# A four-layer streaming trunk on one core: where the first layer's norm comes from, where the convolution's sums lie, and a new table for the planned order

## Chip, core and metric

The kernel runs on one core of a Trainium2 chip. The metric is the device time of one execution in microseconds; lower is better. Shown are the median of three runs and one execution taken apart by the hardware profiler. The engines are TensorE (PE; weight loads are shown apart as PEld), VectorE (DVE), ScalarE (ACT), GpSimd (POOL) and SyncE (SP), which issues the DMAs.

## What is computed

x is 512 frames by 1024 channels in float32. Four layers each add a mixer's output to x: differential attention, a Conformer convolution module, latent attention, and differential attention again. Cut to what the change touches:

```python
def _rms_norm(x, g):
    y = x * lax.rsqrt(jnp.mean(x * x, axis=-1, keepdims=True) + NORM_EPS)
    return y * g

def _conformer_conv(h, w_in, b_in, conv_w, conv_b, ln_g, ln_b, w_out):   # h = _rms_norm(x, g)
    a, b, gate = jnp.split(h @ w_in + b_in, 3, axis=-1)
    u = a * jax.nn.sigmoid(b)
    u = depthwise_causal_conv(u, conv_w) + conv_b        # 31 taps, per channel
    u = jax.nn.silu(_layer_norm(u, ln_g, ln_b))
    return (u * jax.nn.silu(gate)) @ w_out
```

Products of the large matrices are computed in three matmuls with each operand split into a high and a low part (Hh and Hl for x times the norm's gain).

## The kernel before

**Layout.** X holds x with channels on partitions, as 8 blocks of 128 channels by 512 frames. The norm's factor per frame, rs, is not multiplied into Hh and Hl: projections are made of x times the gain, and rs (and its square rs2) is applied to the results, where they leave PSUM or in the sums of squares of q and k.

**The order of the work.** The program is written as nodes (Plan, L363). Each node names its engine, an estimated cost and the buffers that it reads and writes. `Plan.order` (L576) then runs through a model of the engines: at each step, of the nodes that are ready it takes the one that can start first, and among equals the one with the lowest priority number. That number is the place in the program plus a shift, and the table SHIFT (L210 to L353) gives a further shift for each kind of node ("L1_c5.pe=-1835" moves the matmuls of block 5's convolution in layer 1 ahead by 1835 places). What comes out is one fixed sequence of instructions for each engine; on the chip each engine runs its sequence in order and waits on semaphores.

**Buffers.** SLOTS (L53) lists kinds of buffers with their number. A kind marked True is handed out in the order in which the program names them, whoever is ready. For PSUM there are four banks "pp" (True), three banks "x" (False, free for all) and one "o". For SBUF, "mid" has four, "wt" two, "p" two and "big" two.

**Layer 0, `start` (L834).** The four tiles of 128 frames of x are loaded into two "big" buffers, transposed by PE into "x" banks, scaled by the gain into Hh (ACT), copied to X (ACT) and the low part made in Hl (DVE). Then `norm_block` (L881) squares each of the eight blocks of X on ACT (L_sq) and adds them up on POOL (L_sqs); `norm_end` (L895) sums over partitions with matmuls by ones into a bank "o" (L_ss), and a reciprocal square root on POOL gives rs. The rope tables' setup is the next user of the "big" buffers.

**Layer 1, `layer_b` (L1158).** `glu_chunk` (L1204) makes a and b of one or two channel blocks in the four pp banks. The b half is multiplied by R (rs spread over partitions) into SBUF and put through the sigmoid. The a half is multiplied by R out of PSUM into SBUF (into L_ab_v for blocks of kind Y, into u itself otherwise); a second operation adds the bias and multiplies by the sigmoid (L1219, L1223).

KINDS (L30) 'DPDPDYYY' says who sums the 31 taps of each of the eight blocks. D: DVE, 30 operations on a bank "x" (L1236). P: ACT multiplies and POOL adds (L1253). Y: `conv_phase` (L1289) on PE: u is moved by 16 DMAs within SBUF into another layout (L_u4, L1297), DVE builds four weight tiles (L_wa, two buffers "p"), and PE sums into an accumulator of the kind "pp" (L_c). The memset of L_u4 takes the accumulator's bank, and the first matmul comes after the moves.

The gate's channels follow in two chunks of four blocks in the pp banks (L1312), and the program names the three convolution accumulators between them (L1343 to L1347). Behind all stands the LayerNorm over the eight blocks (L_stat, L_mv, L_lnr_y), the transposes back (L_ytr, L1366) and the output projection.

Of the kernel before, what the change touches and what calls it, by code (L numbers as in the profile page):

```python
# [1635 lines left out]
```

## Time and profile before

| | us |
|---|---|
| median of three runs | 1061.58 |
| lowest and highest | 1061.21, 1062.21 |
| the profiled execution | 1064.24 |
| its span, first to last instruction | 1062.4 |
| POOL busy | 216.0 |
| ACT busy | 586.1 |

Lines of the profile read: start, duration, engine, line of the kernel, operation, written tile <- read tiles, shapes and count; in square brackets how long the engine stood idle before, and what ended it. A helper's line stands for all that call it (L465 is every matmul, L519 every DVE operation of two tensors, L531 every operation of a tensor, a scalar and a tensor), so tiles tell more than lines. Layer and buffer numbers are left out of the names: L_c is any layer's c tiles. A row of a group reads: line, engine, operation, tiles, shape and count | busy us in all, mean ns of one | idle us before them and what ended it.

### The profile page before, as it was taken

Reading aid. Unit: us, or ns where it says so; the run is one execution under the profiler, and the core shown is the slowest. Engines: PE = TensorE matmul, PEld = TensorE weight load, DVE = VectorE, ACT = ScalarE, POOL = GpSimd, SP = SyncE. Lnnn points to the kernel's source line nnn. Section 1 sums busy time; section 2 is a strip of 40 time slices with the busy share of each in tenths; the row PEclk is TensorE's granted clock in tenths of the full one; section 3 lists DMA queues with packets and bytes.
Section 4 is the critical chain, followed back from the end, with each engine's and each line's share of the span. In section 5 each row is a group of like instructions: output and inputs, shape, how many; then the busy total and the mean of one; then the engine's idle time right before and its main releaser. Section 6 shows DMA issues by size and latency. Waiting matters only on the chain.

```text
span 1062.4 us, 15183 instructions
## 1 busy us (share of the span) xinstructions
PE 1010.8 (95%) x5212; PEld 847.7 (80%) x5212; DVE 764.4 (72%) x1966; ACT 586.1 (55%) x1226; POOL 216.0 (20%) x142
## 2 busy tenths in 40 slices
PE   8899999998999999798999999999999999999798
PEld 6688788887887887687887778788878888887687
DVE  4767689795669998768344769964683699989651
ACT  6557266657644556653343667753443746666642
POOL 3500000000012899960530001000210000000000
PEclk9999999998999999999999999999999999999899
DMA  7252241314014332220222211112232514423102
GB/s 240 83 138 61 80 119 60 100 48 117 31 51 128 110 104 87 79 91 1 58 91 65 85 50 60 41 38 80 80 100 85 153 41 119 112 68 101 39 20 80
DMA packets 74309, 87.53 MB, mean 82 GB/s; under 512 B 17110, under 2 KB 47702, under 8 KB 74233
## 3 DMA queue, kind: packets, MB, share of 16 engines
q1 hardware_dynamic: 74232, 86.57, 27.5%
q8 instruction: 41, 0.67, 0.3%
q14 instruction: 36, 0.29, 0.1%
HBM read 75.28 MB, written 2.10 MB: 73 GB/s over the span
## 4 chain that ended last, share of the span: by engine, by line
PE 70%; POOL 8%; ACT 8%; DVE 5%; issue 4%; DMA 2%; SPq 2%; DVEq 0%; ACTq 0%; POOLq 0%
PE L_o L465 21%; PE L_qk_a L465 15%; PE L_g_a L465 10%; PE L_v_a L465 7%; PE L_ab_a L465 5%; POOL L_cq L522 4%; POOL L_sqs L522 2%; ACT G L495 1%; SPq L569 1%; PE L_c_a L465 1%; PE L_qk_tr L471 1%; PE L_h7j_sc L465 1%; PE L_h2j_sc L465 1%; PE L_h6j_sc L465 1%; DMA L_setup<-a_lam_k 1%
## 5 line engine op out<-in xcount | busy, mean ns | idle before, releaser
L465 PE MATMUL L_qk_a<-L_qk_w,Hh 128*128 128x512 f32 x512 | 163.1, 400 | 2.6 <-DVE L_qk_T L519 1.3
L465 PE MATMUL L_o<-L_y,L_o_w 128*128 128x512 f32 x576 | 143.3, 398 | 0.3 <-DVE L_y L531 0.2
L465 PEld LDWEIGHTS L_o<-L_y,L_o_w 128*128 128x128 f32 x576 | 105.7, 189 | 21.9 <-DVE L_y L519 0.9
L465 PE MATMUL L_g_a<-L_g_w,Hh 128*128 128x512 f32 x384 | 120.8, 396 | 1.2 <-DVE L_g_w L519 0.5
L745 POOL TENSOR_TENSOR L_h_or_y<-L_h_ov,minus_half 128x4 f32<-128x4 f32 x16 | 17.5, 1093 | 465.9 <-DVE L_h_ov L540 302.3
L465 PEld LDWEIGHTS L_qk_a<-L_qk_w,Hh 128*128 128x128 f32 x512 | 91.9, 189 | 19.6 <-DVE L_qk_T L519 1.5
L465 PE MATMUL L_qk_a<-L_qk_w,Hl 128*128 128x512 f32 x256 | 100.6, 393 | 2.0 <-DVE Hl L531 2.0
L522 POOL TENSOR_TENSOR L_cq<-L_cq,L_ct 128x512 f32<-128x512 f32 x58 | 84.9, 1463 | 24.7 <-ACT L_ct L495 20.7
L465 PE MATMUL L_v_a<-L_v_w,Hh 128*128 128x512 f32 x256 | 82.5, 404 | 2.1 <-DVE L_qk_T L519 2.1
L465 PEld LDWEIGHTS L_g_a<-L_g_w,Hh 128*128 128x128 f32 x384 | 70.2, 188 | 15.9 <-DVE L_g_w L519 0.9
L465 PE MATMUL L_ab_a<-Hh,L_ab_w 128*128 128x512 f32 x256 | 80.1, 391 | 0.0
L465 PE MATMUL L_g_a<-L_g_w,Hl 128*128 128x512 f32 x192 | 75.2, 391 | 0.0
L522 POOL TENSOR_TENSOR L_sqs<-L_sqs,L_sq 128x512 f32<-128x512 f32 x28 | 45.4, 1620 | 130.5 <-ACT L_sq L495 129.1
L531 DVE SCALAR_TENSOR_TENSOR L_c<-L_u,L_tab,L_c 128x512 f32<-128x512 f32 x90 | 65.6, 749 | 1.5
L519 DVE TENSOR_TENSOR L_g_w<-L_g_w_r,L_g_w 128x1024 fp32r<-128x1024 f32 x32 | 43.5, 1360 | 28.9 <-ACT L_g_w L502 28.8
L495 ACT ACTIVATE L_ct<-L_u,L_tab 128x512 f32<-128x512 f32 x60 | 43.0, 722 | 35.1 <-POOL L_cq L522 35.0
L465 PEld LDWEIGHTS L_qk_a<-L_qk_w,Hl 128*128 128x128 f32 x256 | 48.1, 188 | 13.6 <-DVE Hl L531 3.3
L502 ACT CAST L_g_w<-L_g_w_r 128x1024 fp32r<-128x1024 f32 x32 | 33.6, 1050 | 41.7 <-PE L_v_a L465 22.0
L465 PEld LDWEIGHTS L_ab_a<-Hh,L_ab_w 128*128 128x128 f32 x256 | 48.1, 188 | 10.1
L465 PEld LDWEIGHTS L_v_a<-L_v_w,Hh 128*128 128x128 f32 x256 | 46.8, 192 | 11.6 <-DVE L_qk_T L519 2.6
L502 ACT CAST L_qk_w<-L_qk_w_r 128x1024 fp32r<-128x1024 f32 (+1 forms) x33 | 33.7, 1037 | 36.3 <-PE L_o L465 14.6
L465 PE MATMUL L_v_a<-L_v_w,Hl 128*128 128x512 f32 x128 | 50.9, 398 | 0.0
(366 smaller groups left out, 2335.6 us busy)
## 6 DMA issues: line engine op xcount, KB each, us to landing
L_qk_w_r<-a_w_in SPq DMA_DIRECT2D x62, 256.0 KB, 3.0
L_v_w_r<-a_w_in SPq DMA_DIRECT2D x16, 512.0 KB, 3.8
L_g_w_r<-a_w_in SPq DMA_DIRECT2D x16, 512.0 KB, 3.7
L_qk_st<-L_qk_st SPq DMA_DIRECT2D x32, 256.0 KB, 4.3
L_o_w_r<-a_w_out SPq DMA_DIRECT2D x16, 512.0 KB, 3.6
L_ab_w_r<-b_w_in SPq DMA_DIRECT2D x24, 256.0 KB, 3.0
L_g_w_r<-b_w_in SPq DMA_DIRECT2D x8, 512.0 KB, 3.7
L_o_w_r<-b_w_out SPq DMA_DIRECT2D x8, 512.0 KB, 3.7
```

The costliest lines, as they stand in the source:

```text
L465: lambda nc: nc.tensor.matmul(out.real(), a.real(), b.real(), start=start, stop=stop),
L471: emit = lambda nc: nc.tensor.transpose(out.real(), src.real(), ident.real())
L495: nc.scalar.activation(out.real(), src.real(), func, scale=scale.real() if isinstance(scale, View) else scale, **kw)
L502: lambda nc: nc.scalar.copy(out.real(), src.real()), [src], [out])
L519: lambda nc: nc.vector.tensor_tensor(out=out.real(), in0=a.real(), in1=b.real(), op=op), [a, b], [out])
L522: lambda nc: nc.gpsimd.tensor_tensor(out=out.real(), in0=a.real(), in1=b.real(), op=op), [a, b], [out])
L531: self.add("dve", out.n / 960.0 + (0.13 if isinstance(scalar, View) else 0.068), lambda nc: nc.vector.scalar_tensor_tensor(out=out.real(), ...
L569: self.add("sp", 0.45, lambda nc: nc.sync.dma_start(out.real(), src.real()), [src], [out], dma=out.n * 4 * parts)
L745: self.p.add("pool", 0.32 + 0.18 * v.n, lambda nc: nc.gpsimd.tensor_tensor(out=y.real(), in0=v.real(), in1=self.minus_half[:, 0:v.n].real( ...
```

## The change

1. In layer 0 the norm's sums of squares come from the tiles of x as they were loaded, with frames on partitions: four squares of 128x1024 on ACT that add up along the row (the squares themselves are thrown into G, which is not yet in use). The eight squares of X, the POOL adds, the matmuls by ones and their buffer go. Of the copies to X, those of the last two tiles go to DVE.
2. In layer 1 the a half is multiplied by R in place, in its PSUM bank, for all eight blocks; the second operation reads it there. L_ab_v goes.
3. The three convolution accumulators are of the kind "x". The moves of a block now wait until all of its u is written and, from the second block on, until the second of the four matmul groups of the block before.
4. The table SHIFT is another one in all its entries.

```diff
 SHIFT = {k: int(v) for k, v in (x.split("=") for x in """
-L0_g0_a.act=-797 L0_g0_a.pe=27679 L0_g0_w.act=699 L0_g0_w.dve=421 L0_g0_w_r.sp=4 L0_g1_a.act=686 L0_g1_a.pe=-1737
...
@@ start
-                p.copy(self.X[:, k:k + 4, ts_], tr[:, :, :])
+                p.copy(self.X[:, k:k + 4, ts_], tr[:, :, :], "act" if t < 2 else "dve")
...
-        p.shift = 150
-        for k in range(NK):
-            self.norm_block(k, split=False)
-        self.norm_end()
-        p.shift = 0
+        v = self.small(4, "L0_v")
+        for t in range(NT):
+            p.act(self.G[:, t, :], tiles[t // 2][:, t % 2, :], AF.Square, accum=v[:, t:t + 1])
+        p.ts(v, v, 1.0 / D, ALU.mult, EPS, ALU.add)
+        self.norm_root(v)
@@ norm_begin
-        self.sqs = self.buf("wt", name + "_sqs", [P, S])
+        if name != "L0":
+            self.sqs = self.buf("wt", name + "_sqs", [P, S])
@@ norm_end
-        r = self.rsqrt(v, N + "_r")
+        self.norm_root(v)
+
+    def norm_root(self, v):
+        p = self.p
+        r = self.rsqrt(v, self.nname + "_r")
         p.copy(self.rs, r, "dve")
         p.tt(self.rs2, r, r, ALU.mult)
@@ layer_b, glu_chunk
+                a = accs[q][:, :]
+                p.tt(a, a, R[:, :], ALU.mult)
                 if KINDS[b] == "Y":
-                    v = self.buf("mid", f"{N}_v{q}")
-                    scaled(v[:, :], accs[q][:, :], RP[1] == "1" and b >= RPB)
-                    p.stt(by_phase_out(u), v[:, :].split(1, P), vec[:, b, TAPS + 1:TAPS + 2], sg[:, :].split(1, P),
+                    p.stt(by_phase_out(u), a.split(1, P), vec[:, b, TAPS + 1:TAPS + 2], sg[:, :].split(1, P),
                           ALU.add, ALU.mult)
                 else:
-                    scaled(u, accs[q][:, :], RP[1] == "1" and b >= RPB)
-                    p.stt(u, u, vec[:, b, TAPS + 1:TAPS + 2], sg[:, :], ALU.add, ALU.mult)
+                    p.stt(u, a, vec[:, b, TAPS + 1:TAPS + 2], sg[:, :], ALU.add, ALU.mult)
@@ layer_b, conv_phase
+        turn = []
...
-            acc = self.buf("pp", f"{L}_c{b}", [P, 4, 4, 32])
+            acc = self.buf("x", f"{L}_c{b}", [P, 4, 4, 32])
             u4 = self.buf("mid", f"{L}_u4{b}", [P, 4, 8 + P])
-            with p.only_when(bufs=[acc]):
+            with p.only_when(bufs=[acc], reads=(ub[:, b % 2, PAD:PAD + S],), after=turn):
...
+                if g == 1:
+                    turn[:] = [p.last]
```

More of the change, by code (lines that the diff above doesn't have):

```diff
@@ L350 @@
[L350 to L352 removed]
+L0_g0_a.act=5733 L0_g0_a.pe=-1495 L0_g0_w.dve=1051 L0_g0_w_r.sp=-99 L0_g1_a.act=4 L0_g1_a.pe=1821 L0_g1_w.act=-392
+L0_g1_w.dve=1481 L0_g1_w_r.sp=-634 L0_h0_cf.dve=5349 L0_h0_mx.dve=2 L0_h0_or_y.dve=-7476 L0_h0_osq.act=-49
@@ new lines @@
+L0_qk0_w.act=-45489 L0_qk0_w.pool=5391 L0_qk0_w_r.sp=102 L0_qk0_y.dve=-50 L0_qk1_T.dve=-334 L0_qk1_a.pe=10094
+L0_qk1_sq.act=1185 L0_qk1_ss.dve=1548 L0_qk1_st.act=324 L0_qk1_st.dve=-726 L0_qk1_st.sp=-1797 L0_qk1_tr.pe=134
+L0_qk1_v.dve=-6638 L0_qk1_w.act=-348 L0_qk1_w.dve=-142 L0_qk1_w_r.sp=-2396 L0_qk1_y.dve=140 L0_qk2_T.dve=6
+L0_qk2_a.pe=93 L0_qk2_sq.act=-1738 L0_qk2_ss.dve=35614 L0_qk2_st.act=56 L0_qk2_st.dve=-1991 L0_qk2_st.sp=-4402
+L0_qk2_t.dve=1 L0_qk2_tr.pe=3 L0_qk2_w.act=2796 L0_qk2_w.dve=-13677 L0_qk2_w_r.sp=1572 L0_qk2_y.dve=-1588
@@ new lines @@
+L2_c03_sq.act=-398 L2_c03_v.dve=21 L2_c03_y.dve=-287 L2_c0_a.pe=5709 L2_c0_w.act=1128 L2_c0_w.dve=61 L2_g0_a.act=1272
+L2_g0_a.pe=12770 L2_g0_w.act=916 L2_g1_a.act=-1150 L2_g1_a.pe=-3496 L2_g1_w.act=-5434 L2_h0_mx.dve=-3889
+L2_h0_p.act=-73 L2_h0_sc.dve=2317 L2_h0_sc.pe=-367 L2_h0_wtr.pe=39 L2_h1_mx.dve=-72 L2_h1_p.act=-2502
+L2_h1_sc.dve=-124 L2_h1_sc.pe=-1056 L2_h1_wt.act=-469 L2_h1_wtr.pe=960 L2_h2_mx.dve=-514 L2_h2_p.act=-1948
+L2_h2_sc.dve=3507 L2_h2_sc.pe=-10 L2_h2_wt.act=-1949 L2_h2_wtr.pe=-984 L2_h3_mx.dve=291 L2_h3_p.act=-3162
@@ new lines @@
+L2_h3_sc.dve=6340 L2_h3_sc.pe=-10995 L2_h3_wt.act=-2407 L2_h3_wtr.pe=444 L2_h4_mx.dve=51 L2_h4_p.act=-1981
+L2_h4_sc.dve=-6796 L2_h4_sc.pe=-119 L2_h4_wt.act=-1153 L2_h4_wtr.pe=52860 L2_h5_p.act=13637 L2_h5_sc.dve=-11343
+L2_h5_sc.pe=3297 L2_h5_wt.act=1297 L2_h6_mx.dve=3499 L2_h6_p.act=-5134 L2_h6_sc.dve=3900 L2_h6_sc.pe=2947
+L2_h6_wt.act=-15016 L2_h6_wtr.pe=-264 L2_h7_mx.dve=3658 L2_h7_p.act=6622 L2_h7_sc.dve=5282 L2_h7_sc.pe=-3662
+L2_h7_wt.act=-791 L2_h7_wtr.pe=163 L2_kv0_T.act=11 L2_kv0_T.dve=8123 L2_kv0_a.pe=368 L2_kv0_sq.act=-115
@@ new lines @@
+L2_o13.pe=8 L2_o1_w.act=-11046 L2_o1_w.dve=275 L2_o1_w_r.sp=1396 L2_o2.dve=2876 L2_o2.pe=214 L2_o3.dve=31 L2_o3.pe=315
+L2_o4.dve=5161 L2_o4.pe=88 L2_o5.dve=5086 L2_o6.dve=-1030 L2_o6.pe=435 L2_p0_rt.act=-1552 L2_p0_rt.dve=-1273
+L2_p0_rtr.pe=-10064 L2_p0_st.act=146 L2_p0_st.dve=-291 L2_p0_tr.pe=-6773 L2_p1_rt.act=-17 L2_p1_rtr.pe=31
+L2_p1_st.act=198 L2_p1_st.dve=-386 L2_p1_tr.pe=208 L2_p2_rt.dve=9883 L2_p2_rtr.pe=-3586 L2_p2_st.act=1415
+L2_p2_st.dve=1 L2_p2_tr.pe=-3979 L2_p3_rt.act=244 L2_p3_rt.dve=212 L2_p3_rtr.pe=1345 L2_p3_st.act=-53
@@ new lines @@
+L3_h1_p.dve=-234 L3_h1_sc.dve=32 L3_h1_sc.pe=-42 L3_h1_wt.act=-6 L3_h1_wtr.pe=7228 L3_h2_cf.dve=-7976
+L3_h2_mx.dve=-308 L3_h2_or_y.dve=-12021 L3_h2_or_y.pool=1475 L3_h2_ov.dve=-2296 L3_h2_p.act=-58 L3_h2_p.dve=-620
+L3_h2_sc.pe=-1244 L3_h2_wt.act=3325 L3_h2_wtr.pe=-6943 L3_h3_cf.dve=-348 L3_h3_mx.dve=12094 L3_h3_or_y.dve=3
+L3_h3_or_y.pool=2909 L3_h3_osq.act=-972 L3_h3_oss.dve=-571 L3_h3_ov.dve=-781 L3_h3_p.act=-274 L3_h3_p.dve=-5373
+L3_h3_sc.dve=389 L3_h3_sc.pe=636 L3_h3_wt.act=19 L3_h3_wtr.pe=-644 L3_h4_cf.dve=-2707 L3_h4_mx.dve=543
@@ new lines @@
+L3_h6_sc.pe=5340 L3_h6_wt.act=469 L3_h6_wtr.pe=83 L3_h7_cf.dve=4 L3_h7_mx.dve=6354 L3_h7_or_y.dve=1178
+L3_h7_or_y.pool=12272 L3_h7_osq.act=-150 L3_h7_oss.dve=31 L3_h7_ov.dve=38 L3_h7_p.act=-5318 L3_h7_p.dve=804
+L3_h7_sc.dve=280 L3_h7_sc.pe=337 L3_h7_wt.act=4 L3_h7_wtr.pe=-13266 L3_lay.act=9559 L3_lay.sp=-1307 L3_o0.dve=574
+L3_o0.pe=-8330 L3_o00.pe=-186 L3_o01.pe=4982 L3_o03.pe=2194 L3_o0_w.dve=-2508 L3_o0_w_r.sp=264 L3_o1.dve=16240
+L3_o1.pe=236 L3_o10.pe=-1569 L3_o11.pe=8074 L3_o12.pe=5411 L3_o130.pe=410 L3_o131.pe=13131 L3_o1_w.act=965
```

246 lines of the change are left out of this document (105 added, 141 removed).

## Prediction

> **What bounds the kernel now.** I read the page first (busy times), then the clock of the core, then the windows, cut where TensorE pauses.
>
> ```profile
> span 1062.4 us, 15183 instructions
> ...
> PE 1010.8 (95%) x5212; PEld 847.7 (80%) x5212; DVE 764.4 (72%) x1966; ACT 586.1 (55%) x1226; POOL 216.0 (20%) x142
> ```
> ```profile
> core 0: 1062.4 us, clock 0.987
> ```
> ```profile
> 37.00:60.00 23.00, 19.90 (x84) 15.74 (x83) 16.75 (x35) 7.74 (x12) 14.23 (x8) 0.93 0.39 115
> 52.00:56.00 4.00, 4.00 (x12) 3.14 (x13) 2.74 (x11) 0.00 (x0) 1.95 (x1) 0.57 0.33 87
> 248.00:260.00 12.00, 8.98 (x47) 8.24 (x46) 5.15 (x21) 8.41 (x21) 0.00 (x0) 0.72 0.19 65
> 404.00:432.00 28.00, 24.50 (x111) 19.69 (x111) 24.50 (x32) 17.38 (x25) 25.46 (x17) 1.00 0.32 103
> 432.00:459.00 27.00, 23.45 (x101) 18.43 (x102) 15.88 (x33) 18.47 (x27) 25.55 (x19) 1.00 0.18 48
> 459.00:498.00 39.00, 31.90 (x247) 30.57 (x246) 31.17 (x63) 12.06 (x18) 11.43 (x7) 0.91 0.17 57
> 472.00:476.00 4.00, 4.00 (x24) 4.00 (x23) 3.25 (x10) 0.00 (x0) 0.00 (x0) 0.57 0.09 33
> 492.00:496.00 4.00, 3.69 (x15) 3.07 (x16) 4.00 (x9) 1.76 (x3) 0.00 (x0) 0.59 0.02 4
> 976.00:1000.00 24.00, 15.81 (x79) 11.87 (x77) 18.68 (x59) 19.69 (x44) 1.01 (x1) 0.86 0.47 113
> ```
>
> A window row gives its bounds and length, busy time of PE, PEld, DVE, ACT, POOL, the granted clock, and DMA. TensorE is the bound: it idles 1062.4 - 1010.8 = 51.6 us, and its clock was short by 0.013 x 1062.4 = 13.8 us more. No edit removes matmul work worth naming, so the change can only earn out of these 65.4 us. They lie in places: (28 - 24.50) + (27 - 23.45) + (39 - 31.90) = 14.2 us idle plus 0.09 x 39 = 3.5 us of clock in the second half of layer 1 (404 to 498); 3.1 + 0.07 x 23 = 4.7 us in layer 0 (37 to 60); 3.0 + 0.28 x 12 = 6.4 us and 8.2 + 0.14 x 24 = 11.6 us where layers 0 and 3 pass to their output projection. The code edits touch the first two places; the new SHIFT table touches all.
>
> **Layer 0: sums of squares of x as loaded.** The timeline of PE and DVE, the sums' tile, one pause of ACT and one issue of SP:
>
> ```profile
> 47.01 0.72 PE L465 MATMUL L_v_a<-L_v_w,Hh 128*128 128x512 f32 x2 [2.14 <-DVE L_qk_T L519]
> ...
> 51.03 1.05 PE L465 MATMUL L_ss<-ones,L_sqs 128*128 128x1 f32 x8 [0.96 <-POOL L_sqs L522]
> 51.95 0.84 PE L465 MATMUL L_v_a<-L_v_w,Hh 128*128 128x512 f32 x2
> ```
> ```profile
> 54.34 0.17 DVE L505 COPY L_lay<-L_r_y 128x4 f32<-128x4 f32 x1 [0.91 <-POOL L_r_y L745]
> ```
> ```profile
> L522 POOL TENSOR_TENSOR L_sqs<-L_sqs,L_sq x7: 1292/1619/3630, 35.7 to 49.4; 128x512 f32<-128x512 f32 x7
> ```
> ```profile
> 28.55 1.28 ACT L495 ACTIVATE L_qk_sq<-L_qk_a 128x512 f32<-128x512 f32 x2 [6.39 <-PE L_qk_a L465]
> ```
> ```profile
> 9.53 0.38 SPq L563 DMA_DIRECT2D L_setup<-rope_c  x1
> ```
>
> Now eight squares feed seven POOL adds that run from 35.7 to 51.0; TensorE stands 0.96 us before the eight L_ss matmuls and spends 51.95 - 51.03 = 0.92 on them; rs comes at 54.3. Before that it stood 2.14 us for DVE's qk work, whose adds share these microseconds with POOL. The window behind has a granted clock of 0.57, 1.7 us lost. After: no POOL adds, no L_ss, four squares of 128x1024 that sum on ACT. Their prices:
>
> ```profile
> L495 ACT ACTIVATE L_sq<-X 128x512 f32<-128x512 f32 x28 | 16.8, 625 | 7.2 <-POOL L_sqs L522 3.9 <-DVE X L519 1.5 <-DVE L_qk_T L519 0.9
> L502 ACT CAST L_g_w<-L_g_w_r 128x1024 fp32r<-128x1024 f32 x32 | 33.6, 1050 | 41.7 <-PE L_v_a L465 22.0 <-PE L_c_a L465 8.3 <-PE L_qk_a L465 7.4
> L495 ACT ACTIVATION_READ_ACCUMULATOR L_h_osq<-L_o 128x1 f32 x64 | 12.8, 201 | 0.0
> L502 ACT COPY X<-L_tr 128x512 f32<-128x512 f32 x8 | 5.5, 685 | 0.9 <-DVE Hl L531 0.9
> L519 DVE TENSOR_TENSOR L_u<-L_ab_a,L_tab 128x512 f32<-128x512 f32 x5 | 3.4, 680 | 0.0
> ```
>
> ACT gives up 8 x 0.625 = 5.0 us and takes 4 x (1.05 + 0.20) = 5.0: nothing. They need only the loaded tiles, so they fit ACT's pause of 6.39 us before 28.55. Four copies of X go from ACT (4 x 0.685 = 2.7 us) to DVE, priced by its 680 ns row out of PSUM: again 2.7, while DVE is busy only 16.75 of the 23 us behind. The gain is 0.96 + 0.92 + 1.7, and 2.14 if DVE's adds are no longer slowed: 5.7 us. Against it: the squares now hold the tiles of x that the rope setup takes over (its DMA leaves SP at 9.53, with weight loads queued behind it), so two squares, 2.5 us, may push SP; I leave 0.7 for it. I take **5.0**, between 2.6 (the 2.14 stays, and some of the clock) and 5.7.
>
> **Layer 1: convolution sums in the x banks, product in PSUM.** PE's, DVE's, SP's and POOL's timelines, and three groups:
>
> ```profile
> 432.50 0.47 PE L465 MATMUL L_g_a<-Hh,L_g_w 128*128 128x512 f32 x1 [3.00 <-DVE G L519]
> ...
> 439.99 0.50 PE L465 MATMUL L_g_a<-Hh,L_g_w 128*128 128x512 f32 x1 [1.65 <-DVE L_u L558]
> ...
> 446.80 0.50 PE L465 MATMUL L_g_a<-Hh,L_g_w 128*128 128x512 f32 x1 [1.05 <-DVE G L519]
> ...
> 453.32 0.50 PE L465 MATMUL L_g_a<-Hh,L_g_w 128*128 128x512 f32 x1 [0.35 <-DVE G L519]
> ...
> 458.90 10.21 PE L465 MATMUL L_c<-L_wa,L_u 128*128 128x128 f32 x90
> 470.96 11.95 PE L465 MATMUL L_c<-L_wa,L_u 128*128 128x128 f32 x90 [1.85 <-DVE L_wa L519]
> ...
> 492.11 4.65 PE L471 MATMUL L_ytr<-ident,V 128*128 128x128 f32 x20 [4.67 <-DVE V L540]
> ```
> ```profile
> 380.55 0.68 DVE L519 TENSOR_TENSOR L_ab_v<-L_ab_a,L_tab 128x512 f32<-128x512 f32 x1
> ...
> 406.48 1.16 DVE L531 SCALAR_TENSOR_TENSOR L_u<-L_ab_v,L_tab,L_ab_sg 128x512 f32<-128x512 f32 x1
> ...
> 429.89 2.47 DVE L519 TENSOR_TENSOR G<-L_g_a,L_tab 128x512 f32<-128x512 f32 x4
> ...
> 439.90 6.26 DVE L531 SCALAR_TENSOR_TENSOR L_c<-L_u,L_tab,L_c 128x512 f32<-128x512 f32 x8
> ```
> ```profile
> 439.27 21.90 SPq L569 DMA_DIRECT2D L_u<-L_u  x34
> ```
> ```profile
> 465.71 1.29 POOL L522 TENSOR_TENSOR L_cs<-L_cq,L_ct 128x512 f32<-128x512 f32 x1
> ```
> ```profile
> L531 DVE SCALAR_TENSOR_TENSOR L_c<-L_u,L_tab,L_c 128x512 f32<-128x512 f32 x90 | 65.6, 749 | 1.5
> L519 DVE TENSOR_TENSOR L_wa<-L_d,wx 128x1152 f32<-128x1152 f32 x12 | 16.1, 1351 | 4.2 <-PE L_c L465 4.2
> L531 DVE SCALAR_TENSOR_TENSOR L_u<-L_u,L_tab,L_ab_sg 128x512 f32<-128x512 f32 x5 | 6.5, 1309 | 0.8 <-ACT L_ab_sg L495 0.8
> ```
>
> From 432 the three convolution accumulators own three of the four pp banks without a matmul in them; the second gate chunk has one bank and stops at each eviction: 1.65 + 1.05 + 0.35 = **3.05 us**, gone with four banks. Its start waits for four evictions (2.47 us) where one would do: 3/4 of 2.47 = **1.8**. The sums then run last, alone, at the pace of DVE's L_wa, with 1.85 of wait and a dip of 1.7 (472 to 476): **3.5**, gone if they lie between gate matmuls. Behind the last sum stands the LayerNorm: 4.67 and 0.41 x 4 = 1.6 of clock, **6.3**, covered if gate matmuls are left (four banks at 438.34 - 432.50 = 5.84 us each are 23). Sum 14.7. To get it, DVE must do the same work that much sooner: its idle time from 432 to 498 is 11.1 + 7.8 = 18.9 us, of which 4.2 are L_wa waiting for PE. No reserve, so I leave two builds, 2.7, and take **12**. POOL's last sum ends at 467.0 and needs transpose, statistics and the norm (4.67) behind it; the new start of the ytr, 492.1 - 12 = 480, leaves 13 us for that.
>
> The product itself: the multiply (680 ns) writes PSUM instead of SBUF, where the in-PSUM sums of 749 ns are the nearest row, then 749 instead of 1309: eight times between +0.07 and -0.5 us on DVE, beside full TensorE; I take 0. What it adds is a hold: the bank is free after the second operation, which also needs the sigmoid. Block 5's second operation ran 26.4 us after its eviction (381.23 to 407.64). A new order must pull it forward; that also writes its u sooner, so its moves can start sooner.
>
> The moves are SP's: 21.90 / 34 = 0.64 us each, 16 to a block, 10.3 us. By the new wait those of a block stand behind the second group of the block before, and weight loads stand behind them on SP.
>
> The clock bears on 1.7 + 1.7 + 1.6 of these terms: here waits of 2.14, 1.85 and 4.67 us, with thin work near them, were each followed by a window at 0.57 to 0.59. The Trainium skill (TensorE: Matmul & The Clock Gate, "What's actually happening") says that the clock halves after at least one idle window of some 3.4 us. By that rule only the 4.67 would cost clock and the sum would be 3.4 smaller; the trace shows dips behind the shorter ones too, so I keep them.
>
> **The rest of SHIFT.** The same code passes to the output projection at a cost of 6.4 us in layer 0 and 11.6 in layer 3: order alone is worth 5.2 there. A new table moves that either way; I take 0, between -7 and +7.
>
> **Sum.** 5 + 12 = 17. The profiled execution took 1064.24 (span 1062.4 and 1.84 around it) and becomes 1047.2; the median of the three runs is 1061.58, 2.66 lower, and becomes **1044.6, said as 1045**.
>
> **Rivals.**
> 1. *The moves become the chain* (1052, chance 0.18). If block 5's sums only start when DVE's last sum ends (439.90 + 6.26 = 446.2), then half a block (72 x 0.113 / 2 = 4.1), moves 10.3, half 4.1, moves 10.3, a block 8.1 end at 483.1 instead of 487.4: 4.3 instead of 12. For: DVE is busy 24.50 of 28 us before 432. Against: u of block 5 is there early and two L_wa fit in their buffers.
> 2. *The order also closes gaps elsewhere* (1037, 0.15): 7 to 8 us, one passage to an output projection and a bit. For: 65.4 - 17.7 - 4.7 = 43 us lie outside both places. Against: nothing in the code there changes.
> 3. *The order gives back elsewhere* (1055, 0.10): two passages turn as layer 3's is, 10.4 more.
> 4. *Slower* (1066, 0.07): the hold decides. If the second operations of blocks 5 and 6 stay where block 5's is, TensorE works the other three banks (17.5 us) and then waits 26.4 - 17.5 = 8.9, twice, with a dip of 1.7 each: 21.2 lost against 17. It begins to cost at a hold of 17.5 us and turns the sign at some 24 (twice 24.3 - 17.5 and twice 1.7 are 17).
> 5. That the edits miss: rs or the pp banks were not what held TensorE. Then only the table counts, here 0: 1061, 0.05.
>
> **Numbers.** Forecast 0.45. A measurement of this kernel tells about 0.2%, 2 us, from no change. Range 1031 to 1058: its low end is all of layer 1's 17.7, 5.7 in layer 0 and 7 from the table; its high end is 2.6 and 4.3 gained and 3 given back. It holds the forecast and rivals 1 to 3, and leaves out 4, 5 and the tail of 3. Faster 0.88, same 0.05, slower 0.07.
>
> **What would show it.** No L_ss and no POOL adds before 60, rs before 40, clock 1.00 from 37 to 60. L_c matmuls between L_g_a ones, gate banks without waits between them, ytr at some 475 (480 less layer 0's 5). Wrong if PE stands before L_c for L_u DMAs (rival 1), before the next chunk for L_u's second operation (rival 4), or if windows outside both places moved more than 7.

## The result, and the profile after

| | before | after |
|---|---|---|
| median, same chip (us) | 1061.89 (4 runs, 1061.21 to 1062.44) | 1046.71 (4 runs, 1045.98 to 1047.38) |
| ratio, 95% interval | | 0.9838 [0.9808, 0.9869] |
| profiled execution / its span (us) | 1064.24 / 1062.4 | 1047.38 / 1045.6 |
| granted clock | 0.987 | 0.990 |

The change makes the kernel 1.6% faster, and the forecast of 1045 is 1.7 us off. The total came out right. The parts did not: layer 0 gave more than forecast, layer 1 a quarter of it, and work that no edit touches gave the rest. That these misses cancel is luck.

The head of the page after:

```profile
span 1045.6 us, 15204 instructions
...
PE 1006.7 (96%) x5204; PEld 846.2 (81%) x5204; DVE 762.4 (73%) x1970; ACT 585.1 (56%) x1222; POOL 194.8 (19%) x135
```

TensorE's idle time fell from 51.6 to 1045.6 - 1006.7 = 38.9 us; its busy time is 4.1 us shorter, of which some 3 are the better clock (0.003 of the span) and 0.9 the L_ss matmuls that are gone. So the prediction's account (only idle time and clock can be won) holds. Where they were won is read from the windows of the kernel after (bounds and length, busy time of PE, PEld, DVE, ACT, POOL, granted clock, DMA):

```profile
37.00:60.00 23.00, 23.00 (x111) 19.18 (x110) 20.58 (x43) 10.87 (x15) 0.00 (x0) 1.00 0.55 160
239.00:251.00 12.00, 10.26 (x67) 9.20 (x67) 5.11 (x24) 9.71 (x25) 0.00 (x0) 0.86 0.15 47
410.00:440.00 30.00, 29.86 (x187) 26.51 (x186) 28.36 (x38) 17.02 (x25) 27.38 (x20) 1.00 0.27 80
440.00:460.00 20.00, 20.00 (x101) 16.96 (x100) 6.00 (x14) 12.58 (x17) 16.10 (x10) 1.00 0.23 69
460.00:485.00 25.00, 17.64 (x114) 15.85 (x112) 19.54 (x52) 8.61 (x14) 4.60 (x3) 0.80 0.12 41
958.00:984.00 26.00, 19.80 (x104) 15.48 (x102) 20.91 (x68) 22.43 (x48) 2.02 (x2) 0.87 0.31 91
```

Layer 0's stretch from 37 to 60 is full, at full clock. Layer 1's gate matmuls, 410 to 460, run without a gap. But from 460 to 485 TensorE is idle 7.4 us, and the clock is 0.80: what layer 1 lost before among its gate matmuls and its sums is now lost in one place behind them.

A row at a fixed time compares different work once a kernel has gained a few us. So the runs are also compared at equal work: for each kernel, TensorE's busy time is summed over windows of 2 us, less the share that the granted clock withheld, and the time is noted at which the sum reaches a given amount. The table shows that time less the time before; negative is earlier. The measure is not exact: the same matmuls, up to the last one of layer 1's output projection, add up to between 500.5 and 505.0 us in the kernels of these tables, and to 503.3 before and 504.2 after. So an entry is good to a us for the kernel after and to some 2 us for the others; where a reading hangs on less, the start of a matmul that can be named is given beside it.

| work done (us) | 60 | 300 | 400 | 440 | 460 | 500 | 600 | 980 |
|---|---|---|---|---|---|---|---|---|
| place | layer 0, values | end of layer 0 | layer 1, gate begins | gate, sums | last sums, LayerNorm | output projection | layer 2 | end |
| after | -7.1 | -9.4 | -9.0 | -15.6 | -12.6 | -12.4 | -15.7 | -16.2 |

Layer 0's head wins 7.1, the rest of layer 0 2.3, layer 1 3.0 (it had won 6.6 within its gate matmuls and gave 3.2 back behind them), all that follows 3.8. The sum is 16.2. By the traces themselves, the last matmul of layer 1's output projection starts at 530.5 for 542.2, 11.7 sooner, and the span is 16.8 shorter: what follows layer 1 wins some 5, and layer 1 itself 2 to 3.

ScalarE's timeline at the start of the kernel after, and below it VectorE's:

```profile
5.48 1.06 ACT L490 ACTIVATE G<-L_x 128x1024 f32<-128x1024 f32 x1 [3.46 <-DMA L_x<-x]
...
20.84 1.19 ACT L490 ACTIVATE G<-L_x 128x1024 f32<-128x1024 f32 x1
21.79 0.34 ACT L490 ACTIVATION_READ_ACCUMULATOR G<-L_x 128x1 f32 x1
```
```profile
23.80 0.16 DVE L500 COPY L_lay<-L_r_y 128x4 f32<-128x4 f32 x1
```

One square fills ScalarE's first wait for x, three stand in a row before 22; rs is there at 23.8 instead of 54.3. The squares do not lie in the pause before 28.55 that the prediction named, but ahead of it. The tail of layer 1, TensorE's timeline after (start, duration, engine, operation, count, and in brackets the idle time before it and what ended it):

```profile
460.09 1.04 PE L466 MATMUL L_ctr<-ident,L_cs 128*128 128x128 f32 x8
463.19 0.63 PE L466 MATMUL L_ctr<-ident,L_cs 128*128 128x128 f32 x4 [2.06 <-ACT V L497]
463.65 9.83 PE L460 MATMUL L_c<-L_wa,L_u 128*128 128x128 f32 x72
473.32 0.60 PE L466 MATMUL L_ctr<-ident,L_cs 128*128 128x128 f32 x4
478.97 5.77 PE L466 MATMUL L_ytr<-ident,V 128*128 128x128 f32 x24 [5.04 <-DVE V L535]
...
486.80 1.40 PE L460 MATMUL L_o<-L_y,L_o_w 128*128 128x512 f32 x5
```

The sums of blocks 5 and 6 do lie among the gate matmuls now, but block 7's 72 matmuls and the transposes of the four other blocks' sums come behind the last of them. So the statistics end last again, and the LayerNorm stands as bare as before: 5.04 us of wait, 4.67 before.

### The profile page after: what moved, and what is told of

Same layout as the page of the kernel before. It is cut to its first block, busy times and chain, and to the rows that moved or that the text cites. A ratio compares the mean times of both kernels' runs of the same rounds, so it can differ in the third digit from the quotient of the medians.

```text
span 1045.6 us, 15204 instructions
## 1 busy us (share of the span) xinstructions
PE 1006.7 (96%) x5204; PEld 846.2 (81%) x5204; DVE 762.4 (73%) x1970; ACT 585.1 (56%) x1222; POOL 194.8 (19%) x135
## 4 chain that ended last, share of the span: by engine, by line
PE 72%; DVE 14%; ACT 6%; issue 4%; POOL 2%; DMA 1%; SPq 0%; DVEq 0%; ACTq 0%; POOLq 0%
PE L_o L460 20%; PE L_g_a L460 14%; PE L_qk_a L460 12%; PE L_v_a L460 8%; DVE L_c L526 4%; PE L_ab_a L460 2%; PE L_c_a L460 1%; POOL L_cq L517 1%; PE L_c L460 1%; DVE L_qk_T L514 1%; PE L_qk_tr L466 1%; ACT G L490 1%; PE L_kv_a L460 1%; DVE L_qk_t L514 1%; PE L_h3j_sc L460 1%
## 5 line engine op out<-in xcount | busy, mean ns | idle before, releaser
L460 PEld LDWEIGHTS L_qk_a<-L_qk_w,Hh 128*128 128x128 f32 x512 | 92.5, 188 | 16.8 <-ACT G L490 0.3
L517 POOL TENSOR_TENSOR L_cq<-L_cq,L_ct 128x512 f32<-128x512 f32 x58 | 80.2, 1382 | 27.9 <-DMA L_ab_w_r<-b_w_in 21.3
L460 PEld LDWEIGHTS L_ab_a<-Hh,L_ab_w 128*128 128x128 f32 x256 | 47.9, 188 | 15.4 <-DVE L_ab_sg L514 2.0
L517 POOL TENSOR_TENSOR L_sqs<-L_sqs,L_sq 128x512 f32<-128x512 f32 x21 | 32.1, 1528 | 98.3 <-ACT L_sq L490 84.5
L460 PE MATMUL L_ab_a<-Hl,L_ab_w 128*128 128x512 f32 x128 | 49.9, 390 | 0.0
L497 ACT CAST L_o_w<-L_o_w_r 128x1024 fp32r<-128x1024 f32 x32 | 33.6, 1052 | 28.7 <-PE L_g_a L460 16.4
```

Source lines behind the costliest of these rows:

```text
L460: lambda nc: nc.tensor.matmul(out.real(), a.real(), b.real(), start=start, stop=stop),
L497: lambda nc: nc.scalar.copy(out.real(), src.real()), [src], [out])
L517: lambda nc: nc.gpsimd.tensor_tensor(out=out.real(), in0=a.real(), in1=b.real(), op=op), [a, b], [out])
```

## The experiments

The runs were made in groups, each with the kernel before beside it; the ratio to before is what compares runs of different groups.

**The table and the code apart.** Four kernels: each code with each table, and each with none, which leaves the planner its plain order of priorities.

```diff
-SHIFT = {k: int(v) for k, v in ... }   # the code's own table
+SHIFT = {k: int(v) for k, v in ... }   # the other code's table, or none
```

> The code of before with the new SHIFT table. If the gain of 15 us lies in the table (theory 'order'), this alone is faster than before, 1048 to 1056. If the edits carry it and a table fits only the code that it was made for (theory 'edits'), it is slower than before, 1065 to 1085, since its nodes' places are shifted for another program.

> The edits with the table of before. Theory 'order': no faster than before, 1060 or more. Theory 'edits': the start (first 60 us of TensorE work) is still some 4 to 7 us ahead of before and the gate chunks of layer 1 run on four banks, so that stage is ahead too; the whole 1050 to 1070, since a table that does not fit costs elsewhere.

> The code of before with an empty table: what the plain plan gives. Both theories: clearly slower than before, 1085 to 1130. It is the base for the next run.

> The edits with an empty table. Theory 'edits': 6 to 15 us faster than the old code with an empty table. Theory 'order': within 3 us of it.

| code | table | median (us) | ratio to before |
|---|---|---|---|
| old | new | 1078.94 | 1.0113 [1.0066, 1.0161] |
| new | old | 1072.88 | 1.0083 [1.0054, 1.0111] |
| old | none | 1091.53 | 1.0230 [1.0182, 1.0277] |
| new | none | 1102.58 | 1.0341 [1.0302, 1.0380] |

The new table without the edits is slower than before, and so are the edits without the new table: only the two together are faster. The edits under the table of before were to be 4 to 7 us ahead at the start; at work 60 that run is some 4 us behind. The edits under a plain order were to win 6 to 15 us, or to be within 3 us: they lose 11. That loss is in layer 0's start. TensorE's timeline, old code with no table, then new code with no table, then ScalarE of the latter:

```profile
10.15 1.02 PE L324 MATMUL L_qk_a<-L_qk_w,Hh 128*128 128x512 f32 x2
```
```profile
15.50 1.20 PE L324 MATMUL L_qk_a<-L_qk_w,Hh 128*128 128x512 f32 x2
...
27.81 0.80 PE L324 MATMUL L_qk_a<-L_qk_w,Hh 128*128 128x512 f32 x1 [5.00 <-DVE L_qk_w L378]
```
```profile
13.24 1.14 ACT L354 ACTIVATE G<-L_x 128x1024 f32<-128x1024 f32 x1
...
15.29 1.16 ACT L354 ACTIVATE G<-L_x 128x1024 f32<-128x1024 f32 x1
```

With nothing to hold them back, all four squares stand between the evictions that feed the first projection. It begins 5.4 us later, behind transposes of which the last twelve waited 3.21 us for x. TensorE then stands 5.00 us more, for a low part of the weights that VectorE makes only at 27.07, behind the rope tables. So the plain order differs on three engines at once, and how much of the 11 us is the squares' is not shown. Their price on ScalarE is 1.1 to 1.2 us each wherever they are. What was measured as "the change" is therefore edits and table together, and neither has a value of its own. The experiments that follow keep the new table and undo one part each; they contain the damage that a planned order takes when it is not sought anew, and are read stretch by stretch, at equal work.

| work done (us) | 60 | 300 | 400 | 440 | 460 | 500 | 600 | 980 |
|---|---|---|---|---|---|---|---|---|
| after | -7.1 | -9.4 | -9.0 | -15.6 | -12.6 | -12.4 | -15.7 | -16.2 |
| old norm in layer 0 | +0.2 | -3.3 | -2.9 | -9.5 | -6.4 | -6.2 | -9.5 | +6.0 |
| sums in pp banks | -6.6 | -8.8 | -8.6 | -12.1 | -12.4 | -12.4 | -15.5 | -15.4 |
| no wait between blocks' moves | -6.3 | -8.5 | -8.2 | -14.8 | -12.7 | -12.7 | -16.0 | -14.3 |
| product in SBUF (mid) | -6.6 | -8.8 | -9.0 | -10.4 | -4.8 | -4.8 | -8.1 | -7.5 |
| product in SBUF (u), anew | -7.2 | -9.5 | -9.4 | -11.0 | -7.4 | -6.9 | -9.9 | -10.7 |
| product in SBUF (u), same order | -6.5 | -8.7 | +0.6 | -6.1 | -2.8 | -2.8 | -6.2 | -6.8 |
| norm under gate matmuls | -6.8 | -9.0 | -8.7 | -15.3 | -24.6 | -15.6 | -18.9 | -20.0 |
| and y in order | -7.0 | -9.2 | -8.9 | -15.5 | -21.9 | -21.9 | -25.2 | -25.5 |

**Layer 0's norm undone.**

```diff
-        v = self.small(4, "L0_v")
-        for t in range(NT):
-            p.act(self.G[:, t, :], tiles[t // 2][:, t % 2, :], AF.Square, accum=v[:, t:t + 1])
-        p.ts(v, v, 1.0 / D, ALU.mult, EPS, ALU.add)
-        self.norm_root(v)
+        p.shift = 150
+        for k in range(NK):
+            self.norm_block(k, split=False)
+        self.norm_end()
+        p.shift = 0
```

> The changed kernel, with layer 0's norm from squares of X, POOL adds and matmuls by ones as before; the copies of X stay where the change put them. Theory 'edits': the first 60 us of TensorE work lose 3 to 5 of the 7 us that they won (the stand before the sums and the clock dip behind it come back), 1050 to 1053. Theory 'order': they lose nothing, and only scatter of the order within 2 us is seen, 1045 to 1049.

Measured: 1074.39, ratio 1.0115 [1.0084, 1.0145]. At work 60 the gain is gone to the last tenth (+0.2 for -7.1). TensorE's timeline of this run:

```profile
41.85 1.05 PE L460 MATMUL L_ss<-ones,L_sqs 128*128 128x1 f32 x8 [2.69 <-POOL L_sqs L517]
```

The 7.3 us lost at work 60 are more than the 3 to 5 expected, and the whole is 21 us above its range. The stand before L_ss and the clock dip are back (0.93 from 37 to 60), so the 7.1 us are the norm edit's, given a table that places the squares; whether some of them are damage to the order is not told apart here. The further loss, from -9.5 at work 600 to +6.0, lies in layers whose code this run does not touch. An order that no longer fits is what is left to explain it, but it was not looked into.

**The x banks and the wait undone.**

```diff
-            acc = self.buf("x", f"{L}_c{b}", [P, 4, 4, 32])
+            acc = self.buf("pp", f"{L}_c{b}", [P, 4, 4, 32])
...
-            with p.only_when(bufs=[acc], reads=(ub[:, b % 2, PAD:PAD + S],), after=turn):
+            with p.only_when(bufs=[acc]):
```

> The changed kernel with the convolution accumulators of the kind pp again, without the new waits. Theory 'edits': the second gate chunk of layer 1 has one bank again and stops before each of its four blocks, 5 to 7 us later at the end of the gate chunks; at the end of layer 1 the net loss is 3 to 7, 1049 to 1054. Theory 'order': the gate chunks keep their place, 1045 to 1049.

Measured: 1049.97, ratio 0.9881 [0.9859, 0.9902]. TensorE's timeline of this run:

```profile
441.62 0.50 PE L460 MATMUL L_g_a<-Hh,L_g_w 128*128 128x512 f32 x1 [0.79 <-DVE G L514]
447.23 10.21 PE L460 MATMUL L_c<-L_wa,L_u 128*128 128x128 f32 x90
...
477.66 5.92 PE L466 MATMUL L_ytr<-ident,V 128*128 128x128 f32 x24 [4.60 <-DVE V L535]
```

The gate matmuls wait for banks again (3.5 us behind at work 440), the sums run last and alone, and yet at work 500 both kernels stand at -12.4. The banks win their 3 us where they were said to, and it comes back at the end of the layer, because that end is set by the last sum, its statistics and the norm, in both forms alike. By named matmuls the banks are worth 0.5 us over the whole of layer 1: its first matmul starts at 297.4 (after: 299.1), its output projection at 485.6 (486.8). The median, 3 us above after's, lies in the range expected if the banks count, but the profiled execution does not have these 3 us in layer 1.

**Only the wait undone.**

```diff
-            with p.only_when(bufs=[acc], reads=(ub[:, b % 2, PAD:PAD + S],), after=turn):
+            with p.only_when(bufs=[acc], reads=(ub[:, b % 2, PAD:PAD + S],)):
```

> The changed kernel without the wait of a block's moves for the second group of the block before (the accumulators stay in the x banks). If that wait is what leaves the last block's sums alone behind the gate chunks (my rival 1), the moves go out sooner, the tail of 10 us of sums and 5 us of LayerNorm shrinks, and layer 1 is 3 to 8 us shorter, 1039 to 1044. If the order (weight loads between the moves on SP, places in the table) is what puts it last, nothing or little changes, 1045 to 1050.

Measured: 1047.98, ratio 0.9855 [0.9824, 0.9886]: as after. Its TensorE timeline:

```profile
447.18 16.24 PE L460 MATMUL L_c<-L_wa,L_u 128*128 128x128 f32 x144
...
469.03 1.09 PE L466 MATMUL L_ctr<-ident,L_cs 128*128 128x128 f32 x8 [1.97 <-ACT V L497]
475.23 4.59 PE L466 MATMUL L_ytr<-ident,V 128*128 128x128 f32 x20 [5.10 <-DVE V L535]
```

Two blocks of sums now end at 463.4, ten us sooner than after's last, and the transposes take their place as the last thing; the same 2 us and 5 us stand behind them. Three different orders of sums, one bare norm. By named matmuls layer 1 does win 1.9 us: its first starts 1.8 us ahead of after's (297.3), its output projection 3.7 ahead (483.1). The table, good to 2 us here, does not show it. The later layers, whose code this run leaves alone, then take 3.8 us longer than after's; why stays open.

**The product back in SBUF.** In three ways: as before (in a mid buffer for the blocks that TensorE sums), in u itself, so that no mid buffer is held (the edit shown), and in u again with the order of the kernel after kept instruction for instruction.

```diff
-                a = accs[q][:, :]
-                p.tt(a, a, R[:, :], ALU.mult)
                 if KINDS[b] == "Y":
-                    p.stt(by_phase_out(u), a.split(1, P), vec[:, b, TAPS + 1:TAPS + 2], sg[:, :].split(1, P),
+                    p.tt(by_phase_out(u), accs[q][:, :].split(1, P), R[:, :].split(1, P), ALU.mult)
+                    p.stt(by_phase_out(u), by_phase_out(u), vec[:, b, TAPS + 1:TAPS + 2], sg[:, :].split(1, P),
                           ALU.add, ALU.mult)
                 else:
-                    p.stt(u, a, vec[:, b, TAPS + 1:TAPS + 2], sg[:, :], ALU.add, ALU.mult)
+                    p.tt(u, accs[q][:, :], R[:, :], ALU.mult)
+                    p.stt(u, u, vec[:, b, TAPS + 1:TAPS + 2], sg[:, :], ALU.add, ALU.mult)
```

> The changed kernel with the gating product written to SBUF as before. My prediction's step (price 0): 1045 to 1048, and DVE's second operations of some 1.3 instead of 0.75 us where POOL runs. Rival: the hold of the bank costs (0.7 to 1.4 us of wait at each of the two glu chunk ends seen in the changed kernel), then it is faster by 1 to 3.

> The experiment with the product in SBUF once more, but written into u itself, so that it holds none of the four mid buffers; the planner orders it anew. Theory A (the mid buffers: the old product holds one and so delays block 7's buffer and moves): it comes back to the changed kernel, 1046 to 1050 us, with block 7's memset before 450. Rival B (VectorE's own time under GpSimd's additions): it stays at 1053 to 1058, as with the mid buffer. Rival C (neither: any other plan than the one that the table was sought for costs some us): between 1050 and 1060 while the same-order run stays at 1047, with the loss at other places than block 7's moves.

> The changed kernel's own order and buffers, instruction for instruction, but the value half's product with R is written to its place in u in SBUF and the gating operation reads it from there, in place of both in the PSUM bank. No mid buffer is needed for it and nothing is planned anew, so only the operations' own durations and the time at which the bank comes free differ. Theory A (what the product in PSUM saves, 7.6 us in the experiment that took it back, is the mid buffer that the old form holds, or the order that the planner makes of it): 1045 to 1049 us, the same as the changed kernel to 2 us, with the banks free some 1 us earlier in each chunk. Rival B (VectorE's own time: an SBUF operand under GpSimd's additions makes each gating operation 2.0 in place of 1.1 us): 3 to 8 us slower than the changed kernel, 1050 to 1055.

Measured: 1057.00, ratio 0.9938 [0.9916, 0.9960], with the mid buffer; 1053.44, 0.9909 [0.9882, 0.9935], in u; 1053.02, 0.9896 [0.9868, 0.9923], in u and in the same order. Both expectations of the first run missed, no change and 1 to 3 us faster. Within the new order, the product in PSUM, priced at nothing in the prediction, is worth 6 to 11 us (by the ratios 10.6, 7.5 and 6.2). The same-order run says how, since only the operations' own durations, and with them the times at which banks come free, differ in it. VectorE's group of the gating operation, after and then in that run, both from 325 to 410 (busy us, mean ns):

```profile
L526 DVE SCALAR_TENSOR_TENSOR L_u<-L_ab_a,L_tab,L_ab_sg 128x512 f32<-128x512 f32 x8 | 7.1, 892 | 0.0
```
```profile
L528 DVE SCALAR_TENSOR_TENSOR L_u<-L_u,L_tab,L_ab_sg 128x512 f32<-128x512 f32 x8 | 15.1, 1882 | 0.0
```

Eight us more for eight operations. VectorE's and GpSimd's timelines of the same-order run, two of them, and TensorE's two longest waits there:

```profile
352.56 2.76 DVE L528 SCALAR_TENSOR_TENSOR L_u<-L_u,L_tab,L_ab_sg 128x512 f32<-128x512 f32 x1
...
377.85 2.41 DVE L528 SCALAR_TENSOR_TENSOR L_u<-L_u,L_tab,L_ab_sg 128x512 f32<-128x512 f32 x1
```
```profile
352.37 2.40 POOL L519 TENSOR_TENSOR L_ab_w<-L_ab_w_r,L_ab_w 128x1024 fp32r<-128x1024 f32 x1
...
377.33 2.38 POOL L519 TENSOR_TENSOR L_ab_w<-L_ab_w_r,L_ab_w 128x1024 fp32r<-128x1024 f32 x1
```
```profile
376.59 0.50 PE L462 MATMUL L_ab_a<-Hh,L_ab_w 128*128 128x512 f32 x1 [3.40 <-DVE L_ab_sg L516]
...
402.14 0.47 PE L462 MATMUL L_g_a<-Hh,L_g_w 128*128 128x512 f32 x1 [1.87 <-DVE L_ab_sg L516]
```

GpSimd's operation ends at 352.37 + 2.40 = 354.77, the gating operation at 352.56 + 2.76 = 355.32; the second pair ends at 379.71 and 380.26. Both times VectorE ends 0.55 us behind GpSimd, and so does a third, started at 356.57, though the operation alone takes 0.75. That fits an operation that stands until GpSimd is through, not one that runs slowly. With its first operand in PSUM it does not stand, with the same GpSimd operation beside it, in the kernel after:

```profile
354.44 0.74 DVE L526 SCALAR_TENSOR_TENSOR L_u<-L_ab_a,L_tab,L_ab_sg 128x512 f32<-128x512 f32 x1
```
```profile
354.26 2.41 POOL L517 TENSOR_TENSOR L_ab_w<-L_ab_w_r,L_ab_w 128x1024 fp32r<-128x1024 f32 x1
```

VectorE has no room for more, as the sum of the windows from 325 to 410 shows, after and then in the same-order run (length, then busy time of each engine):

```profile
sum 85.00, PE 81.47 PEld 65.46 DVE 83.51 ACT 47.69 POOL 63.72; mean PE 27.16 PEld 21.82 DVE 27.84 ACT 15.90 POOL 21.24
```
```profile
sum 85.00, PE 77.68 PEld 63.04 DVE 83.86 ACT 43.50 POOL 63.08; mean PE 25.89 PEld 21.01 DVE 27.95 ACT 14.50 POOL 21.03
```

So the 8 us reach TensorE through banks that come free later. Layer 1's first matmul starts 1.9 us before after's (297.2 for 299.1), its first gate matmul 3.6 behind (402.1 for 398.5), its y transposes 5.7 behind (484.7 for 479.0): 7.6 us are lost, 5.5 of them ahead of the gate. TensorE's waits from 300 to 412 come to 8.3 us where after has 4.4, and the window behind the longest (377 to 381) has a clock of 0.57, 1.7 us lost.

The theory of the mid buffers fell: without one, the planner's new order still clears block 7's buffer only at 470.3 us, where before 450 was expected, and TensorE waits 2.82 us for that. In the two orders planned anew the gating operations take 11.3 and 10.6 us in place of 7.1, some 4 us of VectorE's time. The rest of their loss is in these orders; how it comes from VectorE's time, if it does, is not shown.

**The norm put under the gate matmuls.** If the order of the last 30 us is what keeps the norm bare, moving it by hand has to win. Nothing but the order of the planned instructions is altered, behind the planner:

```diff
+        self.pull(eng(on("u47"), "sp"), ...)          # block 7's moves before the next weight load
+        self.pull(on("ctr2"), gate[10])
+        self.pull(on("ctr4"), gate[13])
+        self.pull(eng(on("cs3"), "pool"), ...)        # block 3's last sum before the weight splits
+        self.pull(on("ctr3"), gate[19])
+        self.pull(on("ctr1"), gate[19])
+        self.pull(on("c7"), gate[22])
+        self.pull(on("stat", "mv", "v", "lnr_y"), gate[22])
...
```

Here gate[i] is group i of the second gate chunk's 32, and what is pulled goes before it, with all that it depends on.

> The changed kernel with nothing but the order of layer 1's last 30 us altered by hand: in TensorE's order the transposes of the sums of blocks 2, 4, 3 and 1 and then all sums of block 7 go between the matmuls of gate chunk 1, in place of behind them; SyncE issues block 7's 16 moves before any further load of the output weights; GpSimd ends block 3's additions before it splits those weights; VectorE does the statistics and the LayerNorm's scaling before the gate product. Every operation and every buffer stays. Theory A (the end of layer 1 is set by the order: the chain last sums, statistics, LayerNorm stands bare behind TensorE's last matmul, 5.04 us before the y transposes, 2.06 before the third sum transpose, and 1.3 us of lower clock in block 7's sums): 6 to 9 us faster than the changed kernel, 1038 to 1041 us. Rival B (VectorE is what ends last there: its scaling, gate products and y products, some 8.5 us from the root to the output projection, run in one row and only change places): under 3 us, 1044 to 1047. Rival C (block 7's moves land too late for the new place and TensorE stands in mid chunk in place of at its end): no gain or a loss, 1046 to 1050.

Measured: 1043.94, ratio 0.9814 [0.9781, 0.9846]; the profiled span is 1042.3, 3.3 us shorter than after's. That is at rival B's edge and well short of theory A. The timelines of TensorE and then of VectorE and GpSimd in this run say why:

```profile
470.70 4.47 PE L467 MATMUL L_ytr<-ident,V 128*128 128x128 f32 x24
479.65 1.11 PE L467 MATMUL L_ytr<-ident,V 128*128 128x128 f32 x4 [4.48 <-ACT L_yv L491]
...
482.92 1.63 PE L461 MATMUL L_o<-L_y,L_o_w 128*128 128x512 f32 x3
```
```profile
467.94 5.81 DVE L536 TENSOR_SCALAR V<-V,L_mv,L_lnr_y 128x512 f32<-128x512 f32 x8 [1.13 <-POOL L_lnr_y L794]
473.68 2.47 DVE L515 TENSOR_TENSOR G<-L_g_a,L_tab 128x512 f32<-128x512 f32 x4
```
```profile
467.88 2.40 POOL L518 TENSOR_TENSOR L_o_w<-L_o_w_r,L_o_w 128x1024 fp32r<-128x1024 f32 x1
```

The bare norm is gone: the y transposes start with no wait, 8.3 us sooner, and at work 460 the run is at -24.6. Nine of these us are lost again up to work 500. VectorE is late next: the scaling takes 5.81 us for 3.74 in the kernel after, as GpSimd splits weights beside it, the gate product follows, and block 0's y comes third in the planner's row, so the output projection starts at 482.92, only 3.9 us sooner than after.

**And y in the order of its blocks.** Rival B's half was again an order, so it was moved too: GpSimd's split before the norm, half the scaling behind the first two blocks, y from block 0 on.

```diff
+        row = scale[0:4] + tr[0:3] + silu[0:3] + gp + prod[0:2] + cast[0:2] + lo[0:2] + [silu[3]] + gs + [tr[3]]
+        row += scale[4:8] + o[0][0:2] + [tr[4]] + o[1][0:2] + [silu[4]] + prod[2:4] + cast[2:4] + lo[2:4] + w6
...
+        self.place(row, gate[-1])
```

> As the kernel with the LayerNorm under the gate matmuls, and the next 25 us reordered by hand too: block 7's sums two matmul groups later, so that GpSimd's split of the third pair of output weights is done before the LayerNorm and does not run beside VectorE's scaling (5.81 us there in place of 3.74); after the root VectorE scales only the first half, then takes the gate products (their banks are what the output projection writes to), then y of blocks 0 and 1, then the second half; y is made in the order of the blocks, 0 to 7 in place of 1, 3, 0, 4, 5, 7, 2, 6; and TensorE starts the output projection with blocks 0 and 1 between the y transposes. Every operation stays; some buffers change places. Theory A (with the LayerNorm covered, what ended last was VectorE's order of work: the projection began at 482.9 because y of block 0 came third, behind 5.81 us of scaling): the projection begins at 476 to 478, and the time falls by 4 to 7 us to 1037 to 1040 us. Rival B (VectorE is full there whatever its order): the projection begins earlier but stands for later blocks, and no more than 2 us are won, 1041.5 to 1044. Rival C (the moved weight splits and casts collide with it on VectorE's or ScalarE's side, or the output projection then waits for its weights): 1044 to 1050.

Measured: 1036.55 (5 runs, 1036.24 to 1038.70), ratio 0.9753 [0.9731, 0.9776], the fastest here and 9 us below the kernel after by the ratios, with the same operations; it lies just below the range of theory A. TensorE's and VectorE's timelines, and the window of the tail:

```profile
454.95 8.20 PE L462 MATMUL L_c<-L_wa,L_u 128*128 128x128 f32 x72
468.45 2.53 PE L468 MATMUL L_ytr<-ident,V 128*128 128x128 f32 x16
472.76 3.23 PE L462 MATMUL L_o<-L_y,L_o_w 128*128 128x512 f32 x6 [1.78 <-ACT L_y L499]
```
```profile
467.15 1.91 DVE L537 TENSOR_SCALAR V<-V,L_mv,L_lnr_y 128x512 f32<-128x512 f32 x4 [1.13 <-POOL L_lnr_y L850]
```
```profile
460.00:485.00 25.00, 23.09 (x123) 18.79 (x122) 19.91 (x40) 12.59 (x20) 3.65 (x2) 0.93 0.12 40
```

Four scalings take 1.91 us with GpSimd quiet, the projection starts at 472.76 for 486.80, and the window that idled 7.4 us now idles 1.9. Block 7's sums take 8.20 us where they took 9.83. It beats the span that was forecast for this start (476 to 478), and none of it is given back later: -21.9 at work 500, -25.5 at the end, where after has -12.4 and -16.2.

## Why the prediction was right, and where it was wrong

- **What bounds it.** Right. But for L_ss's 0.9 us, TensorE's idle time and clock are all that moved, and each gain or loss that could be placed was found there.
- **Layer 0's norm, 5.0.** Mechanism right, the size 7.1. The four terms, 5.7 in all, were won: the stretch from 37 to 60 has no idle time and a clock of 1.00, and GpSimd has no work in it. The rope setup's DMA did move, as named, by ten us, and cost nothing that shows:

```profile
20.07 0.37 SPq L558 DMA_DIRECT2D L_setup<-rope_c  x1
```

  The 0.7 left for it was not needed. Missing is what the start wins: 1.4 of the 7.1 are there at work 20, but that is not sure, as the other runs with the same start have 0.5 to 1.5 there. That squares "fit ACT's pause" did not come so: one runs while ScalarE waits for x, and the table puts three just ahead of the pause. With plain priorities all four stood in the first projection's way, in a start that lost 11 us.
- **Layer 1's banks, 12.** Wrong. The terms 3.05 and 1.8 for the gate's waits came (a gain of 6.6 from work 400 to 440, the product's share within it). The failed step is "covered if gate matmuls are left", with the 3.5 for the sums and the 6.3 for the norm. Gate matmuls were left, but the planner set them ahead of block 7's sums and of the transposes. Layer 1 wins 3.0 in all. That is nearly rival 1's 4.3 and not its reason: block 7's moves came late, from 442.56 to 459.96 with weight loads between them, but the run without the wait had them early (the last at 443.35) and won 1.9 us in layer 1, nothing in the whole.
- **"I take 0" for the product in PSUM.** Wrong: the step that failed is "beside full TensorE". The mean of 1309 ns was read as the operation's price, and the difference as time that TensorE's work would cover. It is a mixture of 0.75 alone and up to 2.44 us behind GpSimd, so it is set by the order it was measured in. Eight operations took 6.5 + 3.9 = 10.4 us before, take 7.1 now and 15.1 with SBUF operands in the new order; and VectorE was full there, so TensorE had to wait for it. The before kernel's group, by shape, shows it in one row (min, median, max):

```profile
L531 DVE SCALAR_TENSOR_TENSOR L_u<-L_u,L_tab,L_ab_sg x5: 740/752/2437, 335.8 to 383.7; 128x512 f32<-128x512 f32 x5
```

- **The bank held until the second operation** (rival 4). It did not come: the new order runs that operation 3 to 7 us behind the product in every block.
- **The rest of the table, 0.** Zero was wrong and the range of 7 held barely, if at all: -2.3 in the rest of layer 0 and -3.8 behind layer 1, together 6.1 by the table, and some 7 with the 5 that the traces give behind layer 1. That is rival 2's mechanism, which the prediction set on top of layer 1's 12; it came in place of them. The two passages to an output projection are 5 of it. Layer 0's, at 239 to 251 now, loses 1.7 us idle and 0.14 x 12 = 1.7 of clock, where it lost 6.4; layer 3's, at 958 to 984 now, loses 6.2 and 0.13 x 26 = 3.4, where it lost 11.6. Which entries of the table did it was not tried.
- **The sum.** 5 + 12 + 0 was forecast, 7.1 + 3.0 + 6.1 came. It fits within a us by luck: the largest miss, 9 too much in layer 1, was made up by 2 in layer 0 and 6 that had been counted at nothing.
- **What was to show it.** L_ss, the adds, rs, the clock and the gate banks as said. The y transposes start at 478.97, not at 475; this was the sign that layer 1 had not done what it should.

## What to carry to other kernels

When a wait goes, look at what ends the stage, not only at the waits within it: here three forms of the sums ended in the same bare 5 us, until the chain last sum, statistics, norm was itself set ahead of matmuls that could cover it. An edit in a kernel with a searched order has no price of its own; undo it in the same order, instruction for instruction, to see what the operation costs, and with a new order to see what the planner makes of it. And look at the minimum and the maximum of a group before its mean is used as a price.

## What the runs showed of the hardware

- **VectorE behind GpSimd.** An operation of VectorE with two tensors in SBUF, started while GpSimd works on SBUF, waits for GpSimd's operation to end: 2.76 and 2.41 us in place of 0.75, with ends 0.55 us behind GpSimd's. With one of the tensors in PSUM it was not held; the convolution's steps of the same run, most of them beside the same additions, reach 759 ns at most (count, then min, median, max):

```profile
L528 DVE SCALAR_TENSOR_TENSOR L_c<-L_u,L_tab,L_c x90: 720/746/759, 328.7 to 441.9; 128x512 f32<-128x512 f32 x90
```

  In the Trainium skill this is stated (SBUF — State Buffer, "Who interferes with whom"): a VectorE instruction with two SBUF inputs and a GpSimd instruction that reads SBUF contend, and the second to start is blocked until the first is done. By that rule the two ends lie within one operation of each other, and the traces agree.
- **A scaling with one tensor input is held too.** Eight scalings from SBUF to SBUF took 5.81 us with a GpSimd split of 2.40 us running when the first began, and with GpSimd quiet 3.74 in the kernel after and 2 x 1.91 = 3.8 in the last run: 2.0 more, about one GpSimd operation. The same section of the Trainium skill counts such operations among those that can take the shared port; these runs agree.
- **The clock falls behind a stretch that was half busy.** Windows of 4 us of the kernel after:

```profile
460.00:464.00 4.00, 1.94 (x16) 1.64 (x15) 3.97 (x11) 3.68 (x7) 3.16 (x2) 0.97 0.33 121
464.00:468.00 4.00, 4.00 (x24) 4.00 (x24) 2.94 (x10) 0.44 (x1) 0.43 (x1) 0.61 0.41 131
```

  The longest pause in the first was 2.06 us, TensorE worked for 1.94 of the 4 us, and the clock behind it was 0.61: block 7's 72 matmuls took 9.83 us, and 8.20 in the last run, where no pause stood ahead of them. By the rule that the prediction weighed, of the Trainium skill (TensorE: Matmul & The Clock Gate, "What's actually happening"), the clock falls after at least one idle window of some 3.4 us. This pause would have cost nothing by it; the trace does not bear it out. Nor is it the longest pause alone that counts: in layer 0 before, the window at 0.57 (52 to 56) came five us behind the wait of 2.14 that the prediction set it to, and just behind the one of 0.96; TensorE was busy for 1.86 of the 4 us from 44 and 3.04 of the 4 us from 48, at full clock in both.
